# A two-layer decoder step on one core: prompt scores as three 32-row products of split keys and queries in place of one 96-row product of stacked copies

## The chip, the cores and the metric

The kernel runs on one core of a Trainium2 chip. The metric is device time of one call in microseconds, from the first to the last instruction and what lies around them. TensorE (PE in the rows) multiplies matrices; VectorE (DVE), ScalarE (ACT) and GpSimd (POOL) do elementwise work; SyncE (SP) only issues transfers. Each engine runs its own instructions in a fixed order.

## What is computed

The reference is two layers of a decoder, for a prompt of 512 rows and for 8 x 4 sample rows. Each layer has a mixing part of four parallel groups and a gated feed-forward part (FFN):

```python
z = rms_norm(x, g_mix_pre) @ w_in
a, ga, u, vb, q, k, v, xd = split(z)             # 256 columns each
ya = silu(layer_norm(causal_conv31(a * sigmoid(ga))))
vb = layer_norm(gelu(vb), sgu_ln_g, sgu_ln_b)
yb = gelu(u) * (causal_w_128x128 @ vb + sgu_b)   # 4 heads, chunks of 128 rows
p1, p2 = softmax(q1 @ k1.T + bias), softmax(q2 @ k2.T + bias)   # 4 heads, depth 32
yc = rms_norm((p1 - lam * p2) @ v) * attn_sub_g
yd = (windowed_mean(xd) - xd) @ pool_w
x = x + rms_norm(concat(ya, yb, yc, yd) @ w_out)
x = x + ffn(x)
```

Keys and values of the prompt are outputs as well. The sample rows go through the same formulas with a paged cache.

## The kernel before

To keep float32 precision, each dense product is three products of fp32r halves: `hi*hi`, `hi*lo` and `lo*hi`, with `hi` a rounded copy and `lo` the remainder (`split`, `hilo`). The weights are split on the chip, `whi` by ScalarE (L190) and `wlo` by VectorE (L193).

The work of a layer stands in two stages. The mixing stage goes through w_in in blocks of 256 columns in the sequence of a list, `order`: first the convolution's columns (0), then gate (256), keys (1280), queries (1024), values (1536), pooling (1792), and the two gating blocks u (512) and vb (768). Each block is two tiles of 128 columns, and each of those two halves of the prompt, 256 and 288 rows of x. A half is 24 matmuls into one of two PSUM banks called `acc`; an eviction then empties the bank. Between these halves, coroutines put the rest of the work: `conv` and `taps` (60 VectorE instructions of L416 in a layer, the depthwise convolution), `stack`, `attention`, `gating` and `pooling`. A scheduler turns what they record into one fixed sequence per engine.

`stack` prepares the scores. For each of two groups c of 128 columns it transposes keys for the output, splits keys and queries into `qkh` and `qkl` (L474), and copies 32-row pieces of them by 24 transfers (L478) into `st_k` and `st_q`, so that rows 0 to 95 hold (hi, lo, hi) of the keys against (hi, hi, lo) of the queries. `attention` then has 8 units (i, hh) for each c: query tile i, head hh, and both softmax halves m; the score product is `128 x 128(i+1)`, one matmul of 96 rows for each m (two PSUM banks called `s`). VectorE adds the bias and takes the minimum (L501), ScalarE takes the exponential (L503), and three units later `weights` (L511 to L518) combines and transposes the two halves, and `values` multiplies by v into the bank `oT`.

`gating` transposes vb, normalizes it on VectorE (L595), applies gain and offset of the layer norm (L596, L597), and multiplies by the causal weights. `pooling` makes `wn` on VectorE (L632 to L652) and multiplies by pool_w.

The second stage is the product with w_out. Its rows of y are taken in the sequence yd, ya, yb, yc (`W_OUT_ORDER`), its output in eight turns (tile, half of 512 columns) (`W_OUT_TURNS`): the first two turns are half 0 of tiles 0 and 1, the next two half 1 of the same tiles. The work on sample rows and the parameters of the next layer (`params`, with the small loads `lq` at L292 and `lam` at L293 to L297) is put between the turns and into the FFN that follows.

## Time and profile before

| | before |
|---|---|
| time, median of 3 runs | 1456.01 us (1452.26 to 1457.11) |
| the profiled execution's own time | 1448.71 us, span 1446.8 us |
| busy share of the span | PE 95%, DVE 57%, ACT 35%, POOL 18% |
| mean granted TensorE clock | 0.978 |
| mixing stage of layer 0, from the key transposes to the end of the first two w_out turns | 47.05 to 192.29 us |
| the same of layer 1 | 766.64 to 907.40 us |

The table is read from the top: the profiled execution is 7.3 us shorter than the median of the runs, so a sum made on the trace is carried to the median as a difference. PE's busy share is close to the whole; the stretches where it is not are those where something else can shorten or lengthen the call.

### The profile page before, as it was taken

How to read it: one execution, taken by the hardware profiler on the slowest of the kernel's cores; microseconds unless marked ns; L12 is line 12 of the kernel's file. 1: busy time of each engine (PE TensorE's matmuls, PEld its weight loads, DVE VectorE, ACT ScalarE, POOL GpSimd, SP SyncE). 2: the span in 40 equal slices, each digit the busy share in tenths (PEclk: the TensorE clock that was granted, in tenths of full speed). 3: DMA queues.
4: the chain of work that ended last, by engine and by line, in shares of the span. 5: the costliest groups of instructions: out<-in, count | busy, mean ns of one | idle time of the engine just before them, and what ended most of it. 6: DMA issues, size and time to landing. Idle time of an engine off the chain costs nothing.

```text
span 1446.8 us, 22864 instructions
## 1 busy us (share of the span) xinstructions
PE 1372.0 (95%) x9114; PEld 1078.7 (75%) x9114; DVE 823.8 (57%) x1660; ACT 504.7 (35%) x985; POOL 262.7 (18%) x271
## 2 busy tenths in 40 slices
PE   6999787999999999999989988989999999999997
PEld 6987576877666777777689976777776677768775
DVE  4986759866434333333669976778663333333344
ACT  4346634322224321222343474543322332222231
POOL 1000145455300000000220011544442000000003
PEclk9999799999999999999999997999999999999999
DMA  6452134888848752132434521468877496213132
GB/s 206 116 156 73 59 121 145 301 307 297 296 164 254 241 171 77 59 117 106 150 120 119 146 68 58 163 237 281 318 276 266 153 315 220 81 61 114 59 135 91
DMA packets 160091, 242.15 MB, mean 167 GB/s; under 512 B 10444, under 2 KB 118226, under 8 KB 159986
## 3 DMA queue, kind: packets, MB, share of 16 engines
q1 hardware_dynamic: 141410, 173.32, 37.1%
q0 software_dynamic: 18432, 67.12, 12.4%
q8 instruction: 72, 1.18, 0.3%
q14 instruction: 33, 0.27, 0.1%
q10 hardware_dynamic: 144, 0.26, 0.0%
HBM read 222.33 MB, written 12.04 MB: 162 GB/s over the span
## 4 chain that ended last, share of the span: by engine, by line
PE 81%; DVE 11%; ACT 2%; DMA 2%; issue 2%; POOL 1%; SPq 1%; DVEq 0%; POOLq 0%; ACTq 0%
PE acc L126 61%; PE sx L126 12%; PE ps L126 3%; DVE sca L872 2%; PE s L126 1%; DVE cacc L416 1%; DVE p L501 1%; DVE wlo L193 1%; DVE m L1301 1%; PE oT L126 1%; DVE x_t L1294 1%; ACT whi L190 1%; PE ps L516 1%; SPq L478 1%; PE ps L1001 1%
## 5 line engine op out<-in xcount | busy, mean ns | idle before, releaser
L126 PE MATMUL acc<-xhi,whi 128*128 128x512 f32 (+2 forms) x1152 | 405.5, 353 | 3.2 <-ACT whi L190 2.0
L126 PE MATMUL acc<-xhi,wlo 128*128 128x512 f32 (+2 forms) x1152 | 403.4, 351 | 0.2 <-DVE wlo L193 0.2
L126 PE MATMUL acc<-xlo,whi 128*128 128x512 f32 (+2 forms) x1152 | 402.0, 349 | 1.3 <-DVE xlo L238 1.3
L190 ACT CAST whi<-raw 128x1024 fp32r<-128x1024 f32 x178 | 184.3, 1048 | 333.7 <-PE acc L126 292.8
L193 DVE TENSOR_TENSOR wlo<-raw,whi 128x1024 fp32r<-128x1024 f32 x172 | 217.1, 1268 | 128.7 <-ACT whi L190 126.8
L126 PEld LDWEIGHTS acc<-xhi,whi 128*128 128x128 f32 x1152 | 217.1, 189 | 42.2 <-issue 8.0
L126 PEld LDWEIGHTS acc<-xlo,whi 128*128 128x128 f32 x1152 | 217.2, 189 | 31.9 <-issue 4.1
L126 PEld LDWEIGHTS acc<-xhi,wlo 128*128 128x128 f32 x1152 | 216.9, 188 | 31.5 <-issue 4.7
L126 PE MATMUL acc<-whi,h 128*128 128x512 f32 x704 | 226.7, 397 | 0.0
L126 PEld LDWEIGHTS acc<-whi,h 128*128 128x128 f32 x704 | 131.2, 188 | 44.1 <-issue 11.1
L126 PE MATMUL acc<-wlo,h 128*128 128x512 f32 x352 | 138.6, 395 | 0.0
L1276 POOL TENSOR_TENSOR m<-m,g_g_ffn_post 128x512 f32<-128x512 f32 x14 | 20.1, 1437 | 504.9 <-ACT junk L1275 504.9
L989 DVE STREAM_TRANSPOSE kt<-kr 128x1024 f32<-128x1024 f32 x64 | 78.5, 1233 | 27.6 <-DMA kr<-in_cache_k_dram,ik 23.3
L986 POOL DMA_INDIRECT kr<-in_cache_k_dram,ik x64 | 73.8, 1154 | 100.1 <-DVE kt L989 72.2
L416 DVE SCALAR_TENSOR_TENSOR cacc<-hext,pf,cacc 128x512 f32<-128x512 f32 x120 | 85.4, 747 | 0.6
L1345 DVE SCALAR_TENSOR_TENSOR th<-th,acc 128x512 f32<-128x512 f32 (+1 forms) x46 | 29.9, 649 | 87.2 <-PE acc L126 87.0
L126 PEld LDWEIGHTS acc<-wlo,h 128*128 128x128 f32 x352 | 66.1, 188 | 17.6 <-issue 4.5
L174 POOL TENSOR_TENSOR rsw<-rsw,mhalf 128x1 f32<-128x1 f32 (+2 forms) x62 | 39.1, 636 | 202.9 <-DVE rsw L173 189.4
L1016 POOL DMA_INDIRECT vr<-in_cache_v_dram,iv x64 | 63.2, 988 | 57.0 <-PE sx L126 41.2
L1154 DVE SCALAR_TENSOR_TENSOR sth<-sth,ps 128x64 f32<-128x64 f32 x22 | 4.8, 220 | 86.5 <-ACT sth L1153 86.5
L550 POOL TENSOR_TENSOR rse<-e,mhalf 128x8 f32<-128x8 f32 x4 | 8.5, 2130 | 242.7 <-DVE e L548 242.7
L126 PE MATMUL sx<-vr,pt 128*32 128x256 f32 x512 | 49.3, 381 | 0.0
(401 smaller groups left out, 1864.8 us busy)
## 6 DMA issues: line engine op xcount, KB each, us to landing
raw<-in_w_gu_dram SPq DMA_DIRECT2D x44, 1024.0 KB
raw<-in_w_down_dram SPq DMA_DIRECT2D x20, 1024.0 KB
rws<-in_w_gu_dram SPq DMA_DIRECT2D x40, 512.0 KB
raw<-in_w_in_dram SPq DMA_DIRECT2D x16, 1024.0 KB
raw<-in_w_out_dram SPq DMA_DIRECT2D x8, 1024.0 KB
rwo<-in_w_out_dram SPq DMA_DIRECT2D x16, 512.0 KB
rws<-in_w_down_dram SPq DMA_DIRECT2D x16, 512.0 KB
x<-x_t SPq DMA_DIRECT2D x12, 512.0 KB
```

Source lines behind the costliest of these rows:

```text
L126: T.matmul(out, lhsT, rhs, start=start, stop=stop)
L174: G.tensor_tensor(y, v, mhalf[:P, :n], op=ALU.pow)
L190: S.copy(hi, src)
L193: eng.tensor_tensor(lo, src, hi.bitcast(F32), op=ALU.subtract)
L416: V.scalar_tensor_tensor(a, hext[c][:, t:t + SEQ], pf[:, 8 + 2 * t + c:9 + 2 * t + c], a, op0=ALU.mult, op1=ALU.add)
L478: SY.dma_start(s[32 * g:32 * g + 32, jj, :].bitcast(F32), (hi, lo)[seqs[g]][32 * jj:32 * jj + 32, :].bitcast(F32))
L872: V.scalar_tensor_tensor(a[:, c], ext[:, c, :, t:t + 4], pf[:, 8 + 2 * t + c:9 + 2 * t + c], a[:, c], op0=ALU.mult, op1=ALU.add)
L986: G.indirect_dma_start(out=kr, out_offset=None, in_=ck, in_offset=bass.IndirectOffsetOnAxis(ap=ik[:, s, bg:bg + 1], axis=0))
L989: V.transpose(kt, kr)
L1016: G.indirect_dma_start(out=v.rearrange("p t e -> p (t e)"), out_offset=None, in_=cv, in_offset=bass.IndirectOffsetOnAxis(ap=iv[:, s, a:a + ...
L1276: (V if (t, half) == (3, 1) else G).tensor_tensor(m[t][:, hs], m[t][:, hs], gain[:, hs], op=ALU.mult)
L1345: V.scalar_tensor_tensor(th[:, :n], th[:, :n], 0.5, ou[:, :n], op0=ALU.mult, op1=ALU.mult)
```

## The change

Keys and queries no longer go through `stack`. The eviction of their columns (`ev_qk`) writes the fp32r `hi` half by ScalarE straight from PSUM and the `lo` half by VectorE, also from PSUM, into tiles of 128 rows. A score is three products of 32 rows each (hi hi, lo hi, hi lo), accumulated in PSUM, and both `s` banks are taken at once. The key output is transposed by two accumulating fp32r matmuls (`keys_out`). `attention` starts when its group's queries are done, not when all transfers are issued, and waits for the values later. The pooling block is last in `order`; it was ahead of u and vb. The reciprocal and the scale of the softmax are done once for both heads. In `gating`, the gain of the layer norm is folded into the product's eviction, and its offset goes through four small matmuls into the bias tile `bsg`, so L596 and L597 go. `params` loads the gain as two more rows. Two buffer rings are shorter (`PB` 8 for 10, `t512` 3 for 4).

```diff
-PB = 10
+PB = 8
...
+    identr = cp.tile([128, 128], F32R, name="identr")
+    S.copy(identr, ident)
...
+        SY.dma_start(rows[71:73, :], A["sgu_ln_g"][l].rearrange("(c p) -> c p", p=128))
         o = psx(bank)
-        T.transpose(o[:, :71], rows[:71, :], ident[:71, :71])
+        T.transpose(o[:, :73], rows[:73, :], ident[:73, :73])
...
+        V.tensor_copy(pf[:, 77:79], o[:, 71:73])
...
-        def ev_tmp(d, c, f, tag):
+        def ev_qk(nm, c, f):
+
             def ev(o, half):
-                if half == 0:
-                    d[c] = mp.tile([128, SEQ], F32, tag="p", bufs=PB, name=tag)
+                hi, lo = qk[nm, c]
                 hs = slice(256 * half, 256 * half + 256)
-                if tag == "kT":
-                    S.copy(d[c][:, hs], o[:, :256])
+                if nm == "k":
+                    S.copy(hi[:, hs], o[:, :256])
+                    V.tensor_tensor(lo[:, hs], o[:, :256], hi[:, hs].bitcast(F32), op=ALU.subtract)
                 else:
-                    S.activation(d[c][:, hs], o[:, :256], AF.Copy, scale=cst[:, C_QS + c:C_QS + c + 1])
+                    sc = cst[:, C_QS + c:C_QS + c + 1]
+                    S.activation(hi[:, hs], o[:, :256], AF.Copy, scale=sc)
+                    V.scalar_tensor_tensor(lo[:, hs], o[:, :256], sc, hi[:, hs].bitcast(F32), op0=ALU.mult, op1=ALU.subtract)
                 if half == 1:
-                    S.activation(zs[:, f, :], o[:, 256:288], AF.Copy, scale=1.0 if tag == "kT" else -QSCALE)
+                    S.activation(zs[:, f, :], o[:, 256:288], AF.Copy, scale=1.0 if nm == "k" else -QSCALE)
             return ev
 
-        qT = {}
         order = [
             (0, [(0, ev_copy(hext[0], 0, 0.5, 30)), (1, ev_copy(hext[1], 1, 0.5, 30))]),
             (256, [(2, ev_ga(0)), (3, ev_ga(1))]),
-            (1280, [(10, ev_tmp(kT, 0, 10, "kT")), (11, ev_tmp(kT, 1, 11, "kT"))]),
-            (1024, [(8, ev_tmp(qT, 0, 8, "qT")), (9, ev_tmp(qT, 1, 9, "qT"))]),
+            (1280, [(10, ev_qk("k", 0, 10)), (11, ev_qk("k", 1, 11))]),
+            (1024, [(8, ev_qk("q", 0, 8)), (9, ev_qk("q", 1, 9))]),
...
             (1536, "v"),
-            (1792, [(14, ev_copy(dext[0], 14, 1.0, 15)), (15, ev_copy(dext[1], 15, 1.0, 15))]),
             (512, [(4, ev_copy(uv[:, 0], 4)), (5, ev_copy(uv[:, 1], 5))]),
             (768, [(6, ev_copy(uv[:, 2], 6)), (7, ev_copy(uv[:, 3], 7))]),
+            (1792, [(14, ev_copy(dext[0], 14, 1.0, 15)), (15, ev_copy(dext[1], 15, 1.0, 15))]),
...
-        ST = {}
-
-        def stack():
+        def keys_out():
             for c in range(2):
-                st = ST[c] = {}
-
                 o = ps()
                 for t in range(4):
-                    T.transpose(o[:, 128 * t:128 * t + 128], kT[c][:, 128 * t:128 * t + 128], ident)
-                kt = mp.tile([128, 4, 128], F32, tag="t512", bufs=4, name="ktok")
+                    for s in range(2):
+                        mm(o[:, 128 * t:128 * t + 128], qk["k", c][s][:, 128 * t:128 * t + 128], identr, start=(s == 0), stop=(s == 1))
+                kt = mp.tile([128, 4, 128], F32, tag="t512", bufs=3, name="ktok")
                 S.copy(kt, o.rearrange("p (t f) -> p t f", t=4))
                 SY.dma_start(O[2][l, 0].rearrange("(t p) h c d -> p t (h c d)", p=128)[:, :, 128 * c:128 * c + 128], kt)
                 yield
-                for nm, src, seqs in (("k", kT[c], (0, 1, 0)), ("q", qT[c], (0, 0, 1))):
-                    hi = mp.tile([128, SEQ], F32R, tag="t512", bufs=4, name="qkh")
-                    lo = mp.tile([128, SEQ], F32R, tag="t512", bufs=4, name="qkl")
-                    S.copy(hi, src)
-                    V.tensor_tensor(lo, src, hi.bitcast(F32), op=ALU.subtract)
-                    s = yp.tile([128, 4, SEQ], F32R, tag="y", name=f"st_{nm}")
-                    for jj in range(4):
-                        for g in range(3):
-                            SY.dma_start(s[32 * g:32 * g + 32, jj, :].bitcast(F32), (hi, lo)[seqs[g]][32 * jj:32 * jj + 32, :].bitcast(F32))
-                    st[nm] = s
-                    yield
 
         def attention():
-            pb = mp.tile([128, SEQ], F32, tag="pb", name="pb")
-            SY.dma_start(pb, A["c_pbias"])
             y = None
             for c in range(2):
-                st = ST[c]
+                while ("q", c) not in done:
+                    yield
...
+                    sps = [psx("s") for _ in range(2)]
+                    for n, (a, b) in enumerate(((0, 0), (0, 1), (1, 0))):
+                        for m in range(2):
+                            r = slice(64 * hh + 32 * m, 64 * hh + 32 * m + 32)
+                            mm(sps[m][:, :W], qk["q", c][a][r, 128 * i:128 * i + 128], qk["k", c][b][r, 0:W], start=(n == 0), stop=(n == 2))
                     for m in range(2):
-                        sp = psx("s")
-                        mm(sp[:, :W], st["q"][0:96, 2 * hh + m, 128 * i:128 * i + 128], st["k"][0:96, 2 * hh + m, 0:W])
+                        sp = sps[m]
...
-                    V.reciprocal(dn[:, 2:3], dn[:, 1:2])
-                    V.tensor_scalar(dn[:, 3:4], dn[:, 0:1], dn[:, 2:3], nlam, op0=ALU.mult, op1=ALU.mult)
+                    if hh == 0:
+                        d2 = den[:, i]
+                        V.reciprocal(d2[:, :, 2:3], d2[:, :, 1:2])
+                        V.scalar_tensor_tensor(d2[:, :, 3:4], d2[:, :, 0:1], nlam, d2[:, :, 2:3], op0=ALU.mult, op1=ALU.mult)
...
+            o = acc()
+            for h in range(4):
+                mm(o[64 * (h % 2):64 * (h % 2) + 64, 128 * (h // 2):128 * (h // 2) + 128], gr[:, 64 * h:64 * h + 64], wt[:, h, :])
+            V.tensor_tensor(bsg, o[:, :256].rearrange("p (c t) -> p c t", c=2), bsg, op=ALU.add)
...
-                V.tensor_tensor(vn[:, t, :], vn[:, t, :], gr[:, 0, :], op=ALU.mult)
-                V.tensor_tensor(vn[:, t, :], vn[:, t, :], gr[:, 1, :], op=ALU.add)
...
-                V.tensor_tensor(t, o.rearrange("p (n t) -> p n t", n=4),
-                                bsg[:, c:c + 1, :].to_broadcast([128, 4, 128]), op=ALU.add)
+                V.scalar_tensor_tensor(t, o.rearrange("p (n t) -> p n t", n=4), pf[:, 77 + c:78 + c],
+                                       bsg[:, c:c + 1, :].to_broadcast([128, 4, 128]), op0=ALU.mult, op1=ALU.add)
...
-                if c0 == 1024 and i == 1:
-                    active.append(stack())
+                if c0 == 1024:
+                    done.add(("q", i))
+                    if i == 0:
+                        active.append(attention())
+                    else:
+                        active.append(keys_out())
                 if i == "v":
-                    active.append(attention())
+                    done.add("v")
```

The order of instructions follows from it. On PE at the first scores of group 0, before (`st_k`, `st_q` are the stacked copies; the dense rows after the scores are those of the block of values):

```order
L126 MATMUL acc<-xhi,whi 128x256
L126 MATMUL acc<-xlo,whi 128x256
L126 MATMUL s<-st_k,st_q 128x128 x2
L126 MATMUL acc<-whi,xhi 128x256
L126 MATMUL acc<-wlo,xhi 128x256
L126 MATMUL acc<-whi,xlo 128x256
```

After, at the second unit of group 0 (`k0h` and `q0h` are the hi halves of keys and queries of group 0, `k0l` and `q0l` the lo halves, `s_837` and `s_838` the banks of the two m; the block of values opens behind them):

```order
L126 MATMUL s_837<-k0h_243,q0h_247 128x128
L126 MATMUL s_837<-k0l_244,q0h_247 128x128
L126 MATMUL s_837<-k0h_243,q0l_248 128x128
L126 MATMUL s_838<-k0h_243,q0h_247 128x128
L126 MATMUL s_838<-k0l_244,q0h_247 128x128
L126 MATMUL s_838<-k0h_243,q0l_248 128x128
```

The second unit now stands at the place where the first stood, and the first one two half blocks ahead of it; here the three products of one m stand ahead of those of the other; in 6 of the 16 units of a layer the two m alternate.

On VectorE between the first convolution taps, after (`k0l`, `k1l` and `q0l` are evictions of `acc` banks; `cacc` rows are the taps; before, the same stretch holds taps and `wlo` alone, and the `qkl` rows come later):

```order
L395 TENSOR_TENSOR k0l<-acc,k0h 128x256
L425 SCALAR_TENSOR_TENSOR cacc_456<-hext_233,pf_84,cacc_456 128x512 x4
L195 TENSOR_TENSOR wlo<-raw,whi 128x1024
L425 SCALAR_TENSOR_TENSOR cacc_456<-hext_233,pf_84,cacc_456 128x512
L395 TENSOR_TENSOR k1l<-acc,k1h 128x256
L425 SCALAR_TENSOR_TENSOR cacc_456<-hext_233,pf_84,cacc_456 128x512 x4
L195 TENSOR_TENSOR wlo<-raw,whi 128x1024
```

An `acc` bank of keys or queries is now read by VectorE from behind up to four taps and a `wlo`; before, ScalarE alone emptied it.

On PE at the end of the mixing stage, before (`yd`, `ya`, `yb`, `yc` are the four groups' results, `whi` and `wlo` here halves of w_out, `sq` and `rb` the norm of group 1 of the attention):

```order
L126 MATMUL acc<-wt,vn 64x128 x4
L126 MATMUL acc<-whi,yd 128x512
L126 MATMUL acc<-wlo,yd 128x512
...
L126 MATMUL ps<-cst,sq 128x2 x4
L126 MATMUL acc<-whi,yb 128x512
...
L126 MATMUL acc<-whi,yc 128x512
L126 MATMUL ps<-cst,rb 128x128 x4
L126 MATMUL acc<-whi,yc 128x512
```

After (`wn,pw` is the product of pooling, one for each group of 128 channels):

```order
L126 MATMUL ps<-cst,sq 128x2 x4
L126 MATMUL acc<-wt,vn 64x128 x2
L126 MATMUL acc<-wn,pw 128x512
L126 MATMUL acc<-wt,vn 64x128 x8
L126 MATMUL ps<-cst,rb 128x128 x4
L126 MATMUL acc<-whi,yd 128x512
L126 MATMUL acc<-wlo,yd 128x512
...
L126 MATMUL acc<-wn,pw 128x512
L126 MATMUL acc<-whi,yd 128x512
```

Before, the late input of the first two turns is `yc`, which both turns take last; after, it is the second half of `yd`, which both turns take first.

## Rows read from the trace of the kernel before

**Rows 1.** Page: busy time of the engines, share of the span, instructions.

```profile
PE 1372.0 (95%) x9114; PEld 1078.7 (75%) x9114; DVE 823.8 (57%) x1660; ACT 504.7 (35%) x985; POOL 262.7 (18%) x271
```

**Rows 2.** Busy time of each engine by stretch, layer 0.

```profile
core 0: us, PE busy (x) PEld busy (x) DVE busy (x) ACT busy (x) POOL busy (x), PEclk, DMA share, GB/s
40.40:144.80 104.40, 99.01 (x751) 92.76 (x750) 87.65 (x188) 50.69 (x123) 2.66 (x1) 0.98 0.40 115
144.80:189.20 44.40, 32.09 (x187) 24.14 (x186) 29.64 (x90) 24.88 (x47) 9.10 (x12) 0.77 0.14 48
```

**Rows 3.** TensorE's waits from 60 to 195 us (11 rows; total, times, longest).

```profile
PE ps L447 <- ACT pt L518: 4.4, 1, 4.4
PE acc L126 <- ACT whi L190: 3.1, 2, 2.1
...
PE ps L516 <- ACT cacc L449: 0.4, 1, 0.4
```

**Rows 4.** TensorE timeline: score products and what follows them.

```profile
140.09 0.40 PE L126 MATMUL s<-st_k,st_q 96*128 96x256 f32 x2
140.33 0.30 PE L126 MATMUL acc<-xhi,whi 128*128 128x288 f32 x1
...
144.84 0.51 PE L126 MATMUL s<-st_k,st_q 96*128 96x384 f32 x2
145.20 0.60 PE L575 MATMUL acc<-cst,wn 128*128 128x128 f32 x4
...
150.77 1.20 PE L126 MATMUL s<-st_k,st_q 96*128 96x512 f32 x2
151.77 0.63 PE L439 MATMUL ps<-cst,cacc 128*128 128x128 f32 x2
```

**Rows 5.** TensorE timeline: other shapes among dense products.

```profile
97.41 0.39 PE L126 MATMUL acc<-xhi,wlo 128*128 128x256 f32 x1
97.63 0.28 PE L126 MATMUL acc<-xhi,whi 128*128 128x256 f32 x1
...
178.43 0.39 PE L126 MATMUL acc<-wlo,yd 128*128 128x512 f32 x1
178.66 0.62 PE L126 MATMUL acc<-whi,yd 128*128 128x512 f32 x2
...
173.07 1.04 PE L126 MATMUL acc<-wt,vn 128*64 128x128 f32 x16
173.94 0.82 PE L126 MATMUL oT<-pt,vtok 128*64 128x128 f32 x12
```

**Rows 6.** VectorE's groups, layer 0: busy us, mean ns, idle before.

```profile
L416 DVE SCALAR_TENSOR_TENSOR cacc<-hext,pf,cacc 128x512 f32<-128x512 f32 x60 | 42.6, 747 | 0.3
L193 DVE TENSOR_TENSOR wlo<-raw,whi 128x1024 fp32r<-128x1024 f32 x15 | 18.6, 1238 | 2.8 <-ACT whi L190 2.7
...
L512 DVE TENSOR_SCALAR den<-den,lam 128x1 f32<-128x1 f32 x16 | 4.0, 266 | 0.1
...
L597 DVE TENSOR_TENSOR vn<-vn,sgr 128x256 f32<-128x256 f32 x4 | 1.7, 417 | 0.1
```

**Rows 7.** TensorE timeline: marks of the two layers.

```profile
47.05 0.38 PE L465 MATMUL ps<-cst,kT 128*128 128x128 f32 x2
...
80.71 0.30 PE L126 MATMUL s<-st_k,st_q 96*128 96x128 f32 x1 [0.68 <-DMA st_q<-qkl]
...
192.29 0.50 PE L126 MATMUL acc<-whi,yd 128*128 128x512 f32 x1 [2.13 <-ACT whi L190]
...
766.64 0.27 PE L465 MATMUL ps<-cst,kT 128*128 128x128 f32 x1
...
907.40 0.61 PE L126 MATMUL acc<-whi,yd 128*128 128x512 f32 x1 [2.15 <-ACT whi L190]
```

**Rows 8.** VectorE and ScalarE timelines in the w_out stage, layer 0.

```profile
207.75 0.23 DVE L293 TENSOR_TENSOR lq<-lq 128x64 f32<-128x64 f32 x1 [5.39 <-DMA lq<-in_lambda_k_dram]
...
208.36 0.20 ACT L295 ACTIVATE lam<-lam 128x2 f32<-128x2 f32 x1 [6.66 <-DVE lam L294]
```

More of the change, by code (lines that the diff above doesn't have):

```diff
@@ L277, in params @@
         lam_init = 0.8 - 0.6 * math.exp(-0.3 * l)
-        rows = tp.tile([72, 128], F32, tag="prow", name="prow")
+        rows = tp.tile([74, 128], F32, tag="prow", name="prow")
         for i, n in enumerate(("conv_b", "conv_ln_g", "conv_ln_b", "pool_scale")):
@@ L358, in mixing @@
         vtok = mp.tile([128, 4, 256], F32, name="vtok")
-        kT, kh, kl, qh, ql = {}, {}, {}, {}, {}
+        qk = {(nm, c): [mp.tile([128, SEQ], F32R, name=f"{nm}{c}{s}") for s in "hl"] for nm in "kq" for c in range(2)}
+        pb = mp.tile([128, SEQ], F32, name="pb")
+        SY.dma_start(pb, A["c_pbias"])
+        done = set()
         tg = {}
@@ L373, in ev @@
                 if half == 0:
-                    tg[c] = mp.tile([128, SEQ], F32, tag="t512", bufs=4, name="tg")
+                    tg[c] = mp.tile([128, SEQ], F32, tag="t512", bufs=3, name="tg")
                     S.activation(tg[c][:, 0:256], o[:, :256], AF.Tanh, scale=0.5)
@@ L430, in conv @@
                 T.transpose(o[:30, 128 * c:128 * c + 128], hext[c][:, SEQ:SEQ + 30], ident)
-            cn = mp.tile([128, 256], F32, tag="t256", bufs=1, name="cn")
+            cn = mp.tile([128, SEQ], F32, tag="pt", bufs=3, name="cn")[:, :256]
             S.copy(cn[:30], o[:30, :256])
@@ L534, in attention @@
                         if hh == 1:
+                            while "v" not in done:
+                                yield
                             values(i)
                     yield
-                os_ = mp.tile([128, SEQ], F32, tag="t512", bufs=4, name="os_")
-                sq = mp.tile([128, SEQ], F32, tag="t512", bufs=4, name="sq")
+                os_ = mp.tile([128, SEQ], F32, tag="t512", bufs=3, name="os_")
+                sq = mp.tile([128, SEQ], F32, tag="t512", bufs=3, name="sq")
                 S.copy(os_, oT)
@@ L550, in attention @@
                 G.tensor_tensor(r, e2.rearrange("p t h -> p (t h)"), mhalf, op=ALU.pow)
-                rb = mp.tile([128, 4, 2, 64], F32, tag="t512", bufs=4, name="rb")
+                rb = mp.tile([128, 4, 2, 64], F32, tag="t512", bufs=3, name="rb")
                 V.tensor_copy(rb, r.rearrange("p (t h x) -> p t h x", t=4, x=1).to_broadcast([128, 4, 2, 64]))
@@ L564, in gating @@
         def gating():
-            wn = mp.tile([128, 4, 128], F32, tag="t512", bufs=4, name="wn")
+            wn = mp.tile([128, 4, 128], F32, tag="t512", bufs=3, name="wn")
             SY.dma_start(wn, A["sgu_w"][l].rearrange("h t s -> t h s"))
@@ L569, in gating @@
                 SY.dma_start(bsg[64 * (h % 2):64 * (h % 2) + 64, h // 2, :], A["sgu_b"][l, h, :].partition_broadcast(64))
-            gr = mp.tile([128, 2, 256], F32, tag="sgr", name="sgr")
-            SY.dma_start(gr[:, 0, :], A["sgu_ln_g"][l, :].partition_broadcast(128))
-            SY.dma_start(gr[:, 1, :], A["sgu_ln_b"][l, :].partition_broadcast(128))
+            gr = mp.tile([128, 256], F32, tag="sgr", name="sgr")
+            SY.dma_start(gr, A["sgu_ln_b"][l, :].partition_broadcast(128))
             o = acc()
@@ L625, in pooling @@
                 T.transpose(o[:15, 128 * c:128 * c + 128], dext[c][:, SEQ:SEQ + 15], ident)
-            cn = mp.tile([128, 256], F32, tag="t256", bufs=1, name="cn")
+            cn = mp.tile([128, SEQ], F32, tag="pt", bufs=3, name="cn")[:, :256]
             S.copy(cn[:15], o[:15, :256])
```

## The prediction

> **What bounds the kernel now.** I read the page first: TensorE is busy for 95% of the span, VectorE for 57% [rows 1]. These shares hide two kinds of stretch, so I went on to the windows and to TensorE's waits. While the dense products of w_in run (40.4 to 144.8 us in layer 0), TensorE is busy 99.0 of 104.4 us, and VectorE 87.7, which is 84%: TensorE sets the pace, and VectorE has little to spare. From there to the last result of the mixing stage (144.8 to 189.2) TensorE is busy 32.1 of 44.4 us at a granted clock of 0.77, and VectorE 29.6, or 67% [rows 2]. Here neither is full; the tail is a chain through both and through ScalarE. TensorE's waits between 60 and 195 us sum to 19.7 us in eleven rows, the largest on ScalarE's copy `pt` and on the split of w_out [rows 3]; the lower clock costs 0.23 x 32.1 = 7.4 us more. The stage ends, for my count, where w_out's half 1 begins: 192.29 us in layer 0 and 907.40 in layer 1, that is 145.2 and 140.8 us after the key transposes [rows 7]. The FFN is dense and isn't touched. So the change can move two mixing stages and what hangs on them, and no more.
>
> **Scores.** A unit had two products and now has six. From the starts of successive rows one product takes (140.33 - 140.09)/2 = 0.12 us at 256 columns and 0.18 at 384; at 512 it took 0.50 at the low clock, so 0.25 at the full one [rows 4]. For 128 columns I take half of 256's, 0.06. Four more products in each of 4 units of each width (2 groups, 2 heads) make 4 x 4 x (0.06 + 0.12 + 0.18 + 0.25) = 9.8 us a layer. That price assumes that 32 rows cost as much as 96. It can be lower where products of different rows overlap: the 16 products `acc<-wt,vn` of 64 output rows took 0.87 us together, 0.054 each, at the low clock [rows 5], where 128 columns at the rate of the 512-column product would take 0.125 [rows 4]; so halves of the array were filled together there. In the new order only 6 of 16 units alternate the two m, so overlap would give back at most half of 6/16 of three products' time, 0.5 x 6/16 x 14.7 = 2.7 us. I take 9.8 and keep 7.1 as the lower bound.
>
> The Trainium skill ("TensorE: Matmul & The Clock Gate", Part 3) says that matmuls on 32 rows in distinct row groups run at the same time, while a single one with 32 rows takes as long as one with 128. By the first half of it the sum would be 2.7 us a layer lower; by the second it is the one I use. The 64-row columns of the trace agree with overlap in principle; no 32-row product stands in it.
>
> **Shape switches.** Going back from another shape to the dense products costs about 0.1: 97.41 to 97.63 is 0.22 us, where a product of 256 columns takes 0.12 [rows 4, 5]. The scores now stand in some twenty more places in a layer (pairs torn apart, key transposes as matmuls, four products for the bias): +2 us. Its bounds are nothing (before, most of these places interrupted the dense products too) and 8 us, by 40 places that pay 0.1 both ways.
>
> **Start of the attention.** Before, the first scores stood at 80.71 us and waited 0.68 us for transfers [rows 7]. Now they need no transfer, and stand right behind the first halves of keys and queries, some 19 us earlier by the count of dense rows. TensorE doesn't gain there, since it is full; only the waits on `st_q` and on the minimum, some 2 us, can go. All scores are then issued before the dense products end. The last of these moves from 144.8 to 144.8 + 9.8 + 2 - 2 + 1.4 (the three units' old scores that stood behind it, at about 0.46 a unit) = 156.0 us.
>
> **VectorE.** Removed in a layer: L596 and L597, 8 instructions of 0.42, which overlap their neighbours a little: -3.0 [rows 6]; half of the reciprocals and scales, 8 pairs that overlap, the scale 0.27 [rows 6]: -2. Added: the lo halves in eight pieces of 256 columns in place of four of 512, +0.3, and one for `bsg`, +0.4. Together -4.3. VectorE had 87.7 + 29.6 = 117.3 us in the two windows [rows 2] and now has 113.0. If it keeps 84% of the time until 156.0 it has 0.84 x 115.6 = 97.1 behind it; the other 15.9 at 67% take 23.7, so its last result comes at 179.7 (before: 189.2). The bounds: with VectorE never starved, the last pooling group alone follows the dense products (eviction, four sums, a product, a split: about 6 us), 162; with the tail as long as before (47.5 us from 144.8 to 192.3), the stage ends at 203.5.
>
> **End of the stage.** Before, `yc` came last, and w_out's first two turns had all else behind them. Now pooling is last in the sequence and `yd` is first in the turns. The order shows 6 of the 48 products of these turns ahead of the second pooling product, so 42 follow, at 0.228 us each (178.43 to 178.66 [rows 5]): 9.6 us. That ends at 189.3 in place of 192.3: -3.0 in layer 0. Layer 1 runs the same instructions, so I give it the same length, 142.2 from the key transposes, against 140.8: +1.4.
>
> **The stall on `lq`.** In layer 0 VectorE stood idle for 5.39 us at 207.75, for a load of the next layer's parameters, and ScalarE for 6.66 us behind it [rows 8]. Before, two of these four loads stood on SyncE behind a store of `v_s`, which waits for VectorE; in the new order all four stand ahead of it. So I take -5.4 once, with bounds of 0 and -6.7.
>
> **Sample work.** VectorE is free 9.5 us earlier relative to w_out's last turns, and can do part of the sample work that stood behind 192. I take -2.5 a layer, between 0 and -5.
>
> **Sum.** -3.0 + 1.4 - 5.4 - 5.0 = -12.0 us. The profiled execution took 1448.7, and would take 1436.7; the median of the runs is 7.3 above it, so I carry the difference over: 1456.0 - 12.0 = 1444.0 us. The transfers that go (96 in all) and the rings that shrink cost nothing in this sum: SyncE is not what TensorE waits for but in the two rows on `st_q`, and three `t512` tiles are enough once `qkh` and `qkl` are gone.
>
> **Rivals.** *The tail closes up* (chance 0.22). Attention is ahead, so VectorE isn't starved behind 145, TensorE keeps the full clock, and the stage ends near the bound, 162 + 9.6 = 172 us: -20 in layer 0, -16 in layer 1, with the 10 us above -46 at most. For it: nearly all of the tail's waits stand behind attention's second group [rows 3]. Against it: pooling and its norms now have to follow the last dense product. From half of the way to all of it, that is 1410 to 1433, with 1421 in the middle.
>
> *Banks held by VectorE* (0.22; slower). An eviction of keys or queries used one ScalarE instruction; now VectorE reads the bank too, from behind up to four taps and a `wlo`, 4 x 0.71 + 1.24 = 4.1 us [rows 6], where the other bank's 24 products take 24 x 0.12 = 2.9 [rows 4]. TensorE would wait up to 1.2 us for each of eight halves in a layer. VectorE's 84% speaks for it, the order, in which these rows stand close to the first taps, against. It decides from 0.75 us a half and layer (12.0/16) upwards; at 1.2 for each half it gives 1444 + 19 = 1463.
>
> *The tail keeps its length* (0.10, no change). TensorE was full before 144.8, so the 11 us of products are paid there. If half of the tail's chain starts only with the last dense product, the stage ends some 6 us later than I say in each layer, and the call takes 1456. For it: the tail is a chain of waits, not of work. Against: u and vb now come ahead of pooling, so gating starts as early as before.
>
> *Switches are dear* (0.06, no change). If each of some 40 places of a layer pays 0.1 us on the way into 32-row products and again on the way out, that is 8 us a layer in place of 2, and 1444 + 12 = 1456. For it: the return at 97.41 did pay that [rows 5]. Against: the two column halves interleaved at 173.07 paid nothing between them. The Trainium skill ("TensorEngine Tiling (Array Packing)", Key Properties) says that a change of tiling mode drains TensorE; the trace before has no 32-row product to show it.
>
> **Chances.** My forecast 0.40, the closed tail 0.22, banks 0.22, the tail's length kept 0.10, dear switches 0.06. My forecast alone reaches from 1435 to 1452 by the bounds of its terms. The range for 8 in 10 takes in half of the closed tail's and all of the banks': 1421 to 1464. A difference under 0.3% (4.4 us) is about what a measurement of this kernel can't tell from none. Faster by more: 0.22 + 0.40 = 0.62; within it 0.10 + 0.06 = 0.16; slower 0.22.
>
> **What would show it.** Right: first scores near 62 us in layer 0, no wait on a transfer there; 32-row rows of 256 columns spaced 0.12 us; the last dense product of w_in near 156; w_out's half 1 near 189 and 142 us behind the key transposes in layer 1; no idle time of VectorE before `lq`. Wrong: TensorE idle in 45 to 110 us, released by the lo halves or by `wlo` (banks); a stage end under 180 (closed tail) or over 195; scores at 0.2 us or more for 256 columns.

## The result, and the profile after

The changed kernel took 1463.47 us (median of 7 runs, 1461.02 to 1466.94) against 1455.97 of the kernel before in the same session: a ratio of 1.006 with a 95% interval of [1.0044, 1.0075]. It is slower by 7.5 us; I had forecast 12.0 us less. A second measurement, the run called e5 below, gave 1.0062 [1.0048, 1.0076].

The page and the windows of [rows 1, 2], after:

```profile
PE 1397.4 (96%) x9274; PEld 1093.5 (75%) x9274; DVE 820.4 (56%) x1624; ACT 499.4 (34%) x976; POOL 258.5 (18%) x271
```

```profile
40.40:144.80 104.40, 103.64 (x813) 93.86 (x812) 84.09 (x183) 54.33 (x133) 3.64 (x4) 1.00 0.26 84
144.80:189.20 44.40, 32.24 (x180) 23.62 (x179) 33.38 (x74) 20.19 (x37) 11.22 (x11) 0.81 0.25 79
```

TensorE's idle time in the dense stretch went from 5.4 us to 0.8, at a granted clock of 1.00. The tail behind it looks as before: 32.2 of 44.4 us busy at 0.81. But TensorE has 160 more products to run. Its waits between 60 and 195 us, as in [rows 3]:

```profile
PE ps L456 <- DVE xn L450: 4.6, 2, 3.9
PE acc L126 <- DVE wn L655: 4.0, 1, 4.0
PE acc L126 <- ACT yd L349: 1.5, 1, 1.5
PE ps L126 <- ACT sq L542: 1.3, 1, 1.3
PE ps L456 <- ACT pt L518: 0.6, 1, 0.6
PE acc L126 <- DVE wlo L195: 0.2, 1, 0.2
```

The waits fell from 19.7 us to 12.2, and the largest now stand on VectorE's normalized convolution `xn` and on pooling's `wn`. So the change did take waits away, and yet the call is longer. To see where, I cut the call at the starts of five TensorE rows in each profile: where layer 1 begins (`m` transposed), the first dense product of layer 1, the beginning of w_out's half 1 (as in [rows 7]), the first product of the FFN (`sx<-xhi,whi`), and the last product. The marks of before that were not shown yet, and those of after; each list opens with the first dense product of the call, which is used further below:

```profile
13.84 0.35 PE L126 MATMUL acc<-xhi,whi 128*128 128x256 f32 x1
...
735.67 0.58 PE L126 MATMUL acc<-xhi,whi 128*128 128x256 f32 x1
...
960.67 0.36 PE L126 MATMUL sx<-xhi,whi 128*128 128x256 f32 x1
```

```profile
13.47 0.35 PE L126 MATMUL acc<-xhi,whi 128*128 128x256 f32 x1
...
192.54 0.40 PE L126 MATMUL acc<-whi,yd 128*128 128x512 f32 x1
...
736.92 0.58 PE L126 MATMUL acc<-xhi,whi 128*128 128x256 f32 x1
...
918.39 0.40 PE L126 MATMUL acc<-whi,yd 128*128 128x512 f32 x1
...
970.15 0.36 PE L126 MATMUL sx<-xhi,whi 128*128 128x256 f32 x1
```

| stretch, us | before | after | e5 (after again) | e5 - before |
|---|---|---|---|---|
| layer 0: start to w_out half 1 | 192.29 | 192.54 | 194.59 | +2.3 |
| layer 0: from there to the FFN | 58.53 | 53.89 | 53.42 | -5.1 |
| FFN of layer 0 | 475.42 | 479.30 | 477.51 | +2.1 |
| layer 1: head, to the first dense product | 9.43 | 11.19 | 9.68 | +0.2 |
| layer 1: first dense product to w_out half 1 | 171.73 | 181.47 | 181.87 | **+10.1** |
| layer 1: from there to the FFN | 53.27 | 51.76 | 51.75 | -1.5 |
| FFN of layer 1 | 477.46 | 481.56 | 477.24 | -0.2 |
| last product of TensorE | 1438.13 | 1451.71 | 1446.06 | +7.9 |

The profiled execution of before took 1448.71 us and that of after 1462.99, which is twice the medians' difference apart; e5's took 1457.32, in a session in which the median of before was 1448.67. So e5 is the one that stands beside the profile of before, and its last column sums to about the loss that the medians show. The FFN's two lengths scatter by 2 to 4 us between two profiles of one kernel, so nothing is read from them. One stretch is longer by 10 us: the mixing of layer 1. Layer 0's two stretches together are 2.8 us shorter (e5), and the w_out part of layer 1 gives 1.5 us back: from the first dense product of the layer to its FFN, layer 1 took 225.0 us before, 233.2 after and 233.6 in e5. The end of the mixing of layer 1, on TensorE and then on VectorE:

```profile
903.21 1.12 PE L126 MATMUL acc<-wn,pw 128*128 128x512 f32 x2 [3.77 <-DVE wn L655]
905.82 0.80 PE L126 MATMUL acc<-whi,yd 128*128 128x512 f32 x1 [1.49 <-ACT yd L349]
906.42 0.63 PE L126 MATMUL acc<-wlo,yd 128*128 128x512 f32 x1
...
918.16 0.39 PE L126 MATMUL acc<-whi,yc 128*128 128x512 f32 x1
```

```profile
905.80 0.69 DVE L350 TENSOR_TENSOR yd<-wn,yd 128x512 fp32r<-128x512 f32 x1 [2.65 <-ACT yd L349]
```

and before, on VectorE:

```profile
188.48 0.69 DVE L346 TENSOR_TENSOR yc<-os__1975,yc 128x512 fp32r<-128x512 f32 x1 [0.68 <-ACT yc L345]
...
903.59 0.69 DVE L346 TENSOR_TENSOR yc<-os__8388,yc 128x512 fp32r<-128x512 f32 x1 [0.68 <-ACT yc L345]
```

In layer 1 VectorE starts its last result 167.9 us behind the first dense product before (903.59 - 735.67) and 168.9 after (905.80 - 736.92): the new sequence gained it nothing. Behind it TensorE needed 3.8 us before (907.40 - 903.59), for six `yc` products and a wait of 2.15 us on the split of w_out [rows 7]; now it needs 12.6 us (918.39 - 905.80), for the 42 products of the first two w_out turns that stand behind `yd`, with four small transposes of the sample work among them. 1.0 + 8.8 is the 9.7 us of the table. In layer 0 the same form came out even, since VectorE was late there before (it started its last result at 188.48) and now starts it at 181.00. On TensorE, and then on VectorE:

```profile
152.60 0.90 PE L456 MATMUL ps<-cst,xn 128*128 128x128 f32 x3 [3.93 <-DVE xn L450]
161.11 0.29 PE L126 MATMUL acc<-xhi,wlo 128*128 128x288 f32 x1
177.46 2.08 PE L126 MATMUL acc<-wn,pw 128*128 128x512 f32 x2 [3.97 <-DVE wn L655]
181.02 0.79 PE L126 MATMUL acc<-whi,yd 128*128 128x512 f32 x1 [1.49 <-ACT yd L349]
182.04 0.63 PE L126 MATMUL acc<-whi,yd 128*128 128x512 f32 x1
```

```profile
181.00 0.69 DVE L350 TENSOR_TENSOR yd<-wn,yd 128x512 fp32r<-128x512 f32 x1 [3.60 <-ACT yd L349]
```

The 42 products also open slowly. The windows around them, three of layer 0 and one of layer 1:

```profile
177.40:181.00 3.60, 2.08 (x2) 0.50 (x2) 0.01 (x1) 1.33 (x3) 0.00 (x0) 0.50 0.88 284
181.00:184.10 3.10, 3.08 (x7) 2.48 (x8) 1.15 (x4) 3.10 (x4) 2.10 (x1) 0.51 0.94 259
184.10:192.50 8.40, 8.40 (x40) 6.92 (x39) 8.29 (x22) 2.39 (x6) 4.92 (x3) 1.00 0.27 91
...
905.80:911.00 5.20, 5.18 (x12) 4.12 (x13) 3.25 (x5) 3.76 (x4) 4.20 (x2) 0.50 0.95 262
```

Behind the waits on `wn` and `yd` the granted clock is 0.50 to 0.51, the lower of its two levels (1.2 GHz), and the first products are 0.43 apart, not 0.23: seven of them in layer 0, twelve in layer 1. From 184.1 in layer 0 it is full again.

The scores, after (`32x384` is depth x columns; x2 is the two banks; the first three rows are the second unit of group 0, whose order "The change" shows):

```profile
61.81 0.33 PE L126 MATMUL s<-k0h,q0h 32*128 32x128 f32 x2
61.97 0.28 PE L126 MATMUL s<-k0l,q0h 32*128 32x128 f32 x2
62.08 0.28 PE L126 MATMUL s<-k0h,q0l 32*128 32x128 f32 x2
...
82.97 0.35 PE L126 MATMUL s<-k0l,q0h 32*128 32x384 f32 x2
83.14 0.35 PE L126 MATMUL s<-k0h,q0l 32*128 32x384 f32 x2
...
85.59 0.40 PE L126 MATMUL s<-k0l,q0h 32*128 32x512 f32 x2
85.82 0.40 PE L126 MATMUL s<-k0h,q0l 32*128 32x512 f32 x2
...
129.14 0.28 PE L126 MATMUL s<-k1l,q1h 32*128 32x256 f32 x1
129.26 0.27 PE L126 MATMUL s<-k1h,q1l 32*128 32x256 f32 x1
129.46 0.40 PE L126 MATMUL acc<-xlo,whi 128*128 128x288 f32 x1
129.79 0.38 PE L126 MATMUL s<-k1h,q1h 32*128 32x256 f32 x1
```

In these three units the order lists the three products of one m ahead of those of the other, and yet they ran as pairs. A pair takes 0.17 at 384 columns and 0.23 at 512, about as much as one product of 96 rows [rows 4]. Only where another product stands between the two m (the dense one at 129.46) do the products follow one by one, 0.12 each at 256 columns; that is so for all products of a unit in 3 of the 16 units of layer 0 and in 5 of layer 1. And the load of the next layer's parameters, as in [rows 8]:

```profile
198.21 0.22 DVE L297 TENSOR_TENSOR lq<-lq 128x64 f32<-128x64 f32 x1 [4.10 <-DMA lq<-in_lambda_k_dram]
```

### The profile page after: what moved, and what is told of

The parts are those of the page before. It is cut to its first block, busy times and chain, and to the rows that moved or that the text cites. A ratio compares the mean times of both kernels' runs of the same rounds, so it can differ in the third digit from the quotient of the medians.

```text
span 1461.3 us, 22976 instructions
## 1 busy us (share of the span) xinstructions
PE 1397.4 (96%) x9274; PEld 1093.5 (75%) x9274; DVE 820.4 (56%) x1624; ACT 499.4 (34%) x976; POOL 258.5 (18%) x271
## 3 DMA queue, kind: packets, MB, share of 16 engines
q0 software_dynamic: 18432, 67.12, 12.6%
## 4 chain that ended last, share of the span: by engine, by line
PE 79%; DVE 9%; DMA 4%; issue 3%; ACT 2%; POOL 2%; SPq 0%; DVEq 0%; POOLq 0%; ACTq 0%
PE acc L126 61%; PE sx L126 10%; PE ps L126 3%; PE s L126 2%; DMA kr<-in_cache_k_dram,ik 2%; DVE sca L879 2%; DVE wlo L195 1%; PE oT L126 1%; DMA raw<-in_w_in_dram 1%; DVE x_t L1301 1%; DVE m L1308 1%; PE ps L516 1%; PE ps L237 1%; POOL rsw L176 1%; PE ps L1008 0%
## 5 line engine op out<-in xcount | busy, mean ns | idle before, releaser
L195 DVE TENSOR_TENSOR wlo<-raw,whi 128x1024 fp32r<-128x1024 f32 x172 | 216.2, 1262 | 137.6 <-ACT whi L192 127.0
L126 PE MATMUL acc<-whi,h 128*128 128x512 f32 x704 | 226.8, 397 | 0.0
L126 PE MATMUL sx<-kt,qs 128*32 128x128 f32 x1024 | 45.7, 277 | 1.9 <-issue 0.9
```

The lines of the kernel that those rows point to most:

```text
L126: T.matmul(out, lhsT, rhs, start=start, stop=stop)
L195: eng.tensor_tensor(lo, src, hi.bitcast(F32), op=ALU.subtract)
```

## The experiments

All ratios are to the kernel before, measured in the same session (its medians there were 1449.75, 1448.67, 1455.69 and 1454.50 us). Theories stand under letters in the expectations, each told where it is used. "L1 mix" is the stretch of the table that grew: before 171.7, after 181.5 and 181.9.

### Where pooling stands

**e1**: the changed kernel, pooling's block ahead of u and vb again.

```diff
+            (1792, [(14, ...), (15, ...)]),
             (512, [(4, ...), (5, ...)]),
             (768, [(6, ...), (7, ...)]),
-            (1792, [(14, ...), (15, ...)]),
```

> The changed kernel with the pooling block back ahead of u and vb, all else as changed. Theory A (the loss comes from pooling standing last, so that yd, which w_out takes first, is the last result): the w_out half 1 starts 8 us or more earlier in layer 1 than the 918.4 of the changed kernel, and the time falls from 1463 to 1446 to 1454. Theory B (the loss comes from the three score products on TensorE): the time stays at 1459 to 1467.

Measured 1.0004 [0.9985, 1.0022], L1 mix 174.3 us. The wait on `wn` is gone from layer 1; of the tail's waits these are the longest:

```profile
PE ps L448 <- DVE xn L450: 2.8, 1, 2.8
PE acc L126 <- ACT yb L349: 1.6, 1, 1.6
PE ps L857 <- DMA sst<-in_state_conv_dram: 1.2, 1, 1.2
```

Most of the loss goes with this one edit, .0056 of .0060. (Two other edits, e3 and e8 below, take back about as much.)

**e2**: the kernel before, pooling's block moved behind u and vb and nothing else (the reverse of the diff of e1).

> The kernel before with only the pooling block moved behind u and vb. Theory A: slower by the same mechanism, w_out held up by yd, 1464 to 1474. Theory B: 1452 to 1460, as before.

Measured 1.0009 [0.9994, 1.0023], L1 mix 180.2 us: +8.4 in that stretch, with `wn` among the longest waits of layer 1:

```profile
PE ps L447 <- DVE xn L441: 5.3, 2, 4.5
PE acc L126 <- DVE wn L652: 2.3, 1, 2.3
```

So the move alone makes the stretch longer. The call hardly shows it, though in e2's own trace, an execution 3.1 us above its median, the last product comes 5.0 us later than before (1443.10). In this order the `lq` load is waited for at 201.06 us in place of 207.75, and loads that come early are worth 0.2% by themselves (e7); that this hides the rest is argued, not shown.

**e4**: the changed kernel with `W_OUT_ORDER = (0, 1, 2, 3, 4, 5, 6, 7)`, so that the late `yd` is taken last.

> The changed kernel, with w_out taking ya, yb, yc, yd in place of yd, ya, yb, yc. Theory A: 36 of the 48 products of the first two turns can go ahead of the late half of yd, at 0.228 us each 8 us a layer, so 1447 to 1455. Theory B: 1459 to 1467.

Measured 1.0045 [1.0028, 1.0061]. L1 mix falls to 173.3 us, as it should when the 42 products no longer wait, but the part from there to the FFN grows from 51.8 to 56.6 us, and the call gains little. By the medians the order of the rows of y is the smaller part of the fault, and pooling's late place the larger; the stretches don't tell them apart, since mixing and w_out of layer 1 together take 230.0 us in e4 and 229.3 in e1, and e4's profiled execution is the fastest of its eight, 3.1 us under its median.

### The three products

**e3**: the changed kernel with both `s` banks as one tile, so that the two m alternate in all 16 units.

```diff
-                    sps = [psx("s") for _ in range(2)]
+                    sp2 = s_pair()
+                    sps = [sp2[:, m, :] for m in range(2)]
```

> The changed kernel with the two score banks as one tile, so that the products of both m alternate in all 16 units. In the trace of the changed kernel two alternating products of 512 columns took 0.22 us, two serial ones 0.46. Theory B: 10 serial units of a layer save half of their 9 us, 4.5 us a layer, and the time falls to 1452 to 1457. Theory A: the tail sets the end, TensorE's gain is mostly idle time, and the time is 1458 to 1465. One bank pair is held until both minima are taken, which could cost up to 3 us a layer by either theory.

Measured 1.0001 [0.9986, 1.0017], L1 mix 179.4 us. TensorE's time in scores (from the start of each place to the next other product, waits left out) is 9.2 and 9.6 us in the two layers before, 13.7 and 15.9 after, 12.3 and 13.0 here. The call gains more than these 4.3 us, 8.6 by the medians. A part of the gap is the profile's: e3's profiled execution is the slowest of its ten, 2.8 us above their median, and its last product comes 3.2 us earlier than e5's. From what the rest comes I can't say.

**e8**: the changed kernel with the first product of each score alone; the two products with a `lo` half are left out.

```diff
-                    for n, (a, b) in enumerate(((0, 0), (0, 1), (1, 0))):
+                    for n, (a, b) in enumerate(((0, 0),)):
```

> The changed kernel with the first of the three score products alone (the two products with lo halves are left out, so scores are less exact). Theory B: the 64 products that go take 9 us a layer on TensorE, and the time falls by 10 us or more under the changed kernel's, to 0.993 to 0.999 of the kernel before. Theory A: the tail is what sets the end, so half of it or less shows: 1.001 to 1.004.

Measured 1.0013 [0.9999, 1.0027], scores 6.8 and 6.9 us. The two further products cost .0049, 7 us, though TensorE spends 16 us on them: less than half reaches the end. L1 mix is still 178.7 us, so products are 3 of the 10 us by which that stretch is longer.

**e6**: e1 and e3 together.

> The changed kernel with the pooling block ahead of u and vb and with the two m alternating in all units. If the serial products and the pooling block cost time each by itself: 0.992 to 0.997 of the kernel before (4 us a layer less than with the pooling block alone). If both only act through the tail that pooling closes: 0.998 to 1.002.

Measured 1.0002 [0.9991, 1.0014], no better than either. L1 mix is the shortest but one, 170.7, but the part behind it takes 58.4 us. There TensorE waits for a load of the sample rows' state:

```profile
906.65 0.40 PE L863 MATMUL ps<-cst,sst 120*128 120x120 f32 x2 [3.17 <-DMA sst<-in_state_conv_dram]
```

So 3.2 of the 6.7 us by which this part is longer than in e5 went to a transfer (e13 has a wait of 3.1 us for the same load). For the rest no cause is shown.

### The loads and VectorE's savings

**e5**: the changed kernel once more, for its ratio and for the scatter of its FFN.

> The changed kernel once more, unchanged, so that it is timed beside the others on one chip and has a second profile. Theory A (mixing stage: the pooling block last holds w_out up by 7 us in layer 1): again 1.004 to 1.008 of the kernel before, with w_out's half 1 near 192 us and 190 to 193 us after the start of layer 1, and FFN stages of 475 to 478 us as in the other runs. Theory C (the FFN stages were 4 us longer each for good: TensorE idle at the gathered keys and a lower clock): FFN stages of 479 to 482 us again.

Measured 1.0062 [1.0048, 1.0076], FFNs 477.5 and 477.2 us, where the first profile had 479.3 and 481.6. A slower FFN as a cause falls.

**e7**: the kernel before with the four `lq` loads first in `params`.

```diff
+        lq = tp.tile([128, 4, 32], F32, tag="lq", name="lq")
+        for i, n in enumerate(("lambda_q1", "lambda_q2", "lambda_k1", "lambda_k2")):
+            SY.dma_start(lq[:, i, :], A[n][l, :].partition_broadcast(128))
```

> The kernel before with the four small lq loads issued ahead of the other parameter loads, nothing else. If the stall on lq (5.4 us in layer 0) is worth its length: 0.995 to 0.998. If it is hidden, since the w_out stage is bound by other VectorE work: 0.999 to 1.001.

Measured 0.9980 [0.9969, 0.9991]: the loads are worth 3 us.

**e11**: e7 with the folded gain, the `bsg` products and the merged reciprocal of the change; stacks and the old sequence stay.

> The kernel before with the lq loads first and the changed kernel's savings on VectorE (gain and offset of the gating norm folded, one reciprocal and scale for both heads), with the stacked copies and the old sequence of blocks. If these savings are worth their 4 us a layer in the tail: 0.993 to 0.996 of the kernel before. If they are hidden: 0.997 to 0.999, as with the lq loads alone.

Measured 0.9956 [0.9939, 0.9973] (1448.89 us against 1455.69): this kernel beats both. The parts of the change that spare VectorE and load early are good, by 6 to 7 us. Its trace has the gain in layer 0 alone: from the first dense product to the FFN, layer 0 takes 226.8 us in place of 237.0, and layer 1 228.4 in place of 225.0. In layer 1 VectorE starts its last result 171.4 us behind the first dense product, 3.5 later than before, in spite of the savings; why is open.

### The sample work

**e9** and **e10**: the kernel before and the changed one with `for t in range(1, 2)` in the convolution of the sample rows, which leaves 29 of its 30 further taps out (58 small VectorE instructions a layer).

> The kernel before without 29 of the 30 later taps of the sample rows' convolution (58 small VectorE instructions of 0.16 us a layer are left out). In all runs so far the FFN starts 9 to 11 us after the last such tap. Theory D (VectorE's sample work sets the end of the w_out stage): 0.990 to 0.995 of the kernel before. Theory E (w_out's own products and the norms behind them set it): 0.998 to 1.000.

> The changed kernel with the same 58 instructions left out. Theory D (the change makes the sample taps late, and these the FFN): the gap to e9 is 3 us or less, so 0.991 to 0.997 of the kernel before. Theory E (the change makes w_out late, and this the FFN): the gap to e9 stays at 6 to 9 us.

Measured 1.0076 [1.006, 1.0091] and 1.0078 [1.0062, 1.0093]: less work, and both slower. The FFNs took 487 to 491 us; their order of instructions is another one than in the kernel before, and in e9 TensorE has waits in the first FFN that the kernel before has not:

```profile
PE acc L126 <- issue: 1.7, 4, 0.8
PE sx L126 <- DMA vr<-in_cache_v_dram,iv: 1.0, 1, 1.0
```

These waits are 2.7 of the 12.5 us by which that FFN is longer. So the call decides nothing on the taps. The stretches say more: the part from w_out's half 1 to the FFN is 4.0 and 4.1 us shorter in e9 than before, and 6.0 and 4.3 shorter in e10 than in e5, which speaks for the taps lying on the way to the FFN in both kernels.

**e12**: the changed kernel with the sample work recorded at high priority.

```diff
-                    if next(fl, 0) == 0:
+                    with tc.high_priority(URG):
+                        over = next(fl, 0) == 0
+                    if over:
```

> The changed kernel with the sample rows' flows recorded at high priority. In the order this moves the sample transposes ahead of 8 products of w_out and the taps ahead of the second x_t, in layer 0 alone; in layer 1 they stay. Theory D: 1 to 3 us faster than the changed kernel, 1.004 to 1.006 of the kernel before. Theory E: 1.005 to 1.007.

Measured 1.0039 [1.0025, 1.0054]. It gains about 0.2%, with an uncertainty as large, but L1 mix stays at 181.5 us. By this run the sample work is a smaller share of the loss.

### Do the prices add?

**e13**: e1 with the edit of e8 (one product of three). **e14**: e11 with pooling's block last.

> The changed kernel with the pooling block ahead of u and vb again, and with the first score product alone (the two products with a lo half are left out). Theory F: what remains slower is the sum of two separate prices, pooling last (.0058 by the runs of pooling back and of the change on one chip) and the two further products (.0049), and both are gone here: .9955 of before, as the kernel before with early loads and the folded gain had (.9956). Theory G: each price is one of lost room in the tail, which the other gives back, so that the two don't add: .999 to 1.001, as either alone.

> The kernel before with the four loads first, the folded gain, the merged reciprocal, and the pooling block moved last; stacks and their transfers stay. Theory F: pooling last costs .0058 of whatever it is put into: .9956 + .0058 = 1.0014 of before. Theory G: with VectorE's savings in place the move costs little: .996 to .998. The move alone into before gave 1.0009 with the loads early by themselves; the loads alone .9980.

Measured 0.9977 [0.9966, 0.9988] and 0.9999 [0.9987, 1.0012], between the two theories both times. L1 mix is 169.1 us in e13 and 181.1 in e14. The two ways from before to after are then, in 0.01% of the time, each step with an uncertainty of some 20:

| step | pooling moved first | pooling moved last |
|---|---|---|
| loads and savings of VectorE (before to e11) | -44 | -44 |
| pooling last | +43 (e11 to e14) | +56 (e1 to after) |
| scores from split keys, one product | +14 (e14 to e8) | +21 (e11 to e13) |
| the two further products | +49 (e8 to after) | +27 (e13 to e1) |
| sum | +62 | +60 |

The first way's steps at the end are read against e5 (+62), the second's against the first measurement (+60). Pooling last costs 0.09% from before to e2, 0.29 from e7 to e2 (whose loads differ as well), 0.36 from e13 to e8, and 0.43 and 0.56 in the table; the two products cost 0.27 to 0.49%. These two outweigh the savings, and their shares depend on what they are put into: e1, e3 and e8 each take back most of the loss by one edit (.0056, .0059 and .0049), so the call alone names no single cause.

What pooling's place does is told by the stretch. In all 14 profiles with every tap, the sequence sets the stretch of layer 1. With pooling ahead of u and vb it took 169.1 to 175.2 us (before, e1, e6, e7, e11, e13). With pooling last and `yd` first it took 178.7 to 181.9 (after, e2, e3, e5, e8, e12, e14). e4, with pooling last and `yd` last, has 173.3. Four pairs differ by pooling's place alone:

| pair | VectorE's last result, us behind the first dense product | from its start to half 1 | L1 mix | L1 mix and w_out |
|---|---|---|---|---|
| before, e2 | 167.9, 167.4 | 3.8, 12.8 | +8.4 | +6.7 |
| e11, e14 | 171.4, 169.1 | 3.8, 12.0 | +5.9 | +2.6 |
| e13, e8 | 164.9, 165.9 | 4.2, 12.8 | +9.6 | +2.5 |
| e1, after | 168.5, 168.9 | 5.8, 12.6 | +7.1 | +3.9 |

VectorE's last result moves by -2.3 to +1.0 us; what stands behind it grows by 7 to 9 us, and the w_out part gives back 2 to 7 us of the longer mixing.

## Why the prediction was wrong

**The step that failed** is the end of the stage, and most of all in layer 1: "Layer 1 runs the same instructions, so I give it the same length". That gave the stage of layer 1 +1.4 us; measured from the first dense product it grew by 9.7 (e5: 10.1). Both terms of the end were too short there. *VectorE's last result*: the forecast's 179.7 of layer 0, carried to layer 1 by the key transposes, puts its end 132.7 us behind them, 5.0 earlier than before (903.59 + 0.69 - 766.64 = 137.6). Counted from the first dense product it came 1.0 later. VectorE had not been late in layer 1: before, it started its last result 167.9 us behind the first dense product, against 174.6 in layer 0 (188.48 - 13.84), and TensorE's wait on `pt`, 4.4 us in layer 0 [rows 3], was 0.4. In e11, with the savings and the early loads alone, it didn't come earlier there either. *The products behind it*: from VectorE's start the forecast has 10.3 us (its own 0.7 and 9.6 for the products), and they took 12.6, with twelve at the low clock. 6.0 + 2.3 is the 8.3 us between +1.4 and +9.7.

That the two layers take the same length turned out nearly right: after, the stage takes 179.1 and 181.5 us from the first dense product to half 1 (e5: 181.0 and 181.9), where before it took 178.5 and 171.7. The length itself was wrong. Counted from the same marks, the forecast was 175.5 in layer 0 and 173.2 in layer 1 (the key transposes, by which it counts, stood 33.2 us behind the first dense product in layer 0 and 31.0 in layer 1). So the change took away the lead that layer 1 had had.

**Layer 0**: forecast -3.0, measured +0.2 and +2.3. The form was right (last `yd`, 42 products, half 1 at 192.5 where I said 189.3). VectorE's last result was forecast for 179.7 and ended at 181.7. The 42 products were sized at 9.6 us at the full clock and took 11.5 (181.02 to 192.54; they open with ScalarE's half of `yd`, 0.7 us before VectorE's ends), as the first seven ran at the low clock; the last dense product stood at 161.1, not 156.0, behind transposes that wait 3.93 us for `xn`.

**Stall on `lq`**: forecast -5.4, timed alone -3 (e7; in its trace the first layer's mixing and w_out are 5.2 us shorter). The loads are earlier, but VectorE is too: it waits 4.10 us for them at 198.21 in place of 5.39 at 207.75. **Sample work**: with it I had -7.9 for layer 0 and -2.5 for layer 1 behind the stage's end; measured -5.1 and -1.5 (e5). Together these two are 3.8 us of the 19.9 between forecast and e5's trace; the two tails are 5.3 and 8.7, the FFNs and the head of layer 1 2.1.

**Scores**: the term was 9.8 us a layer and was 4.5 and 6.3. I had looked for overlap only where the order alternates the two m; the trace shows it wherever no other product stands between them, also where the order lists three of one m first. The price for 128 columns, half of 256's, was too small: a pair took 0.11 (61.97 to 62.08), nearly the 0.12 that one product of 256 columns takes. The Trainium skill ("TensorE: Matmul & The Clock Gate", Part 3 and "Why this matters for your kernels") says that matmuls whose operands lie in distinct groups of 32 rows run concurrently, and a single one takes as long as one of 128 rows. The trace agrees with both: 0.23 for a pair of 512 columns, 0.12 for a single one of 256. Since the scores lie in the stretch that TensorE fills, they were oversized without being the error; a smaller price made the miss larger. Two readings of the trace of before were wrong. The 16 `acc<-wt,vn` products stand in a stretch of full clock, not of the low one, so that their 0.054 us each doesn't show an overlap by the comparison made there. And the trace has products of 32 rows, though small ones of the sample work:

```profile
29.60 0.43 PE L235 MATMUL ps<-cst,xp 32*128 32x32 f32 x4
...
173.00:174.00 1.00, 1.00 (x24) 1.00 (x20) 0.00 (x0) 0.27 (x1) 0.00 (x0) 1.00 0.99 365
```

**Rivals.** "Banks held by VectorE" gave 1463 us, and the time is 1463.5, but its mechanism is not there: between 60 and 195 us no wait of TensorE stands on a lo half, and on `wlo` 0.2 us. Its number was right by accident, and since my range reached to 1464 for its sake alone, the time lies inside the range by luck. The tail did not close up (end at 192.5, not under 180). "The tail keeps its length" is nearest to layer 0; for layer 1 no rival had it growing by 10 us. The drain at a change of tiling that the Trainium skill names ("TensorEngine Tiling (Array Packing)", Key Properties) is not told apart here: the first product of a place of scores takes 0.05 to 0.1 more than the next ones (0.16 for 0.11 at 61.81), as shapes did before [rows 5].

**Right**: no wait on transfers at the first scores (they stand at 54.3, 8 us earlier than my 62), and, by the call, VectorE's savings (e11), though in layer 0 alone.

**Open**: why e3 gains more than its products spare; why layer 1's w_out stage gives back a part of a shorter mixing stage in e1, e4, e6 and e13 (in e6 and e13 the load of `sst` is 3 us of it, the rest isn't shown); why the call of e2 is hardly longer; and how much of the loss is late sample work. In the changed kernel its transposes stand on TensorE behind 34 of the 42 products (916.33 us), and VectorE waits for them:

```profile
916.75 0.42 DVE L343 BATCH_NORM_STATS2 bn<-ps 32x6 f32<-32x256 f32 x1 [3.16 <-PE ps L820]
```

e12 speaks for a share of about 0.2%; by e9 and e10 the taps are 4 to 6 us of the w_out part in both kernels, which doesn't say how much of the difference is theirs.

## What to carry to other kernels

Don't carry the gain of a tail from one layer to the next because the instructions are the same: read for each which engine ends last, whether it was late, and what stands behind its last result. A late producer belongs where little waits for it; moved last with its product taken first, it puts a whole group of products on the path (here 42: 12 to 13 us behind the last result, where 4 to 6 stood). Price a bundle's parts one by one, since here a bundle that lost 0.6% held a part that gained 0.4%.

## What the runs showed of the hardware that was not expected

Two 32-row products in different row groups (32-row slices of the tiles) ran together although TensorE's order lists three of one before those of the other: 0.11 us for a pair of 128 columns at 61.97 and 0.23 for one of 512 at 85.59. So the listed order is not the order of the starts there: the other m's first product is listed fourth and started with the first. After waits of 3.97 and 1.49 us TensorE ran seven products at a granted clock of 0.51 without waiting, and at 1.00 behind them; after waits of 3.77 and 1.49 us in layer 1 it ran twelve at 0.50.
